# 64x64 products of a chunked delta rule on four quarters of the TensorE array, with half of the heads held on the other partitions

## The chip, the core and the metric

One core of a Trainium2 chip runs the whole program. Its engines work side by side and are told here by the names the profile uses: PE (TensorE matmuls; PEld are its weight loads), DVE (VectorE), ACT (ScalarE), POOL (GpSimd), and SP, which here only issues DMAs. The metric is the device time of one execution in microseconds, lower is better. The kernel before takes 1697.08 us, the median of three runs between 1696.71 and 1698.99.

## The reference

One layer of a decoder: 256 prompt tokens and 8 x 4 sample tokens (288 columns together) go through one wide projection, a gated convolution, a gated DeltaNet mixer with 8 heads of 128, merge gates, an output projection, and a feed-forward of width 8192, all in fp32. The part that the change touches is the chunked delta rule of the prompt, 4 chunks of 64 tokens for each head:

```python
M = jnp.where(strict, jnp.einsum('nbhid,nbhjd->nbhij', kb, kc) * decay, 0.0)
T = lax.linalg.triangular_solve(eye + M, jnp.broadcast_to(eye, M.shape),
                                left_side=True, lower=True, unit_diagonal=True)
u = T @ (vc * bc)
w = T @ (kb * jnp.exp(gcum)[..., None])
attn = jnp.einsum('nbhid,nbhjd->nbhij', qc, kc) * decay
...
def step(S, xs):
    qd, kd, u_c, w_c, a_c, gl = xs
    v_new = u_c - w_c @ S
    o = qd @ S + a_c @ v_new
    S = S * jnp.exp(gl)[..., None] + jnp.einsum('bhcd,bhce->bhde', kd, v_new)
    return S, o
```

M, T and attn are 64x64 for each chunk and head; S is 128x128 for each head.

## The kernel before

**The main stream.** Every large weight matrix is read in blocks of 512 KB. A block is split into a rounded part `hi` (ACT, line 179) and a remainder `lo` (DVE, line 186, recorded at line 140, the line of the helper `tt`), three blocks ahead of its use, and PE then issues 24 matmuls of 288 or 290 columns (lines 206 to 208), which the text calls big matmuls. All of this is in program order; there is no scheduler that moves work.

**The side work.** The gates, the delta rule `gdn(G)` for the heads 4G to 4G+3, and the decode step `sample()` are generators. Before each block's 24 big matmuls the main loop lets `side()` run to its next `yield`, and then, if there is one, the generator in `aux`. Whatever these issue to PE stands between two blocks of big matmuls, and PE takes it in that order. So every `yield` marks one block of distance.

**Tiles of the delta rule.** The four heads of a group are hh = 0 to 3, par = hh % 2 and p = hh // 2. `rows[par]` is partitions 0-63 or 64-127: a head with par = 0 keeps its 64 tokens on the lower half, one with par = 1 on the upper. `q` numbers chunk and p (q = 2c + p), 8 in all, so that a [128, 8, 64] tile holds the 64x64 matrices of 4 chunks and 4 heads.

**The steps that matter here**, for each of the two groups:

- Lines 1033 to 1040: the products K K^T and K Q^T into two banks, 32 matmuls.
- `pairs` (lines 1089 to 1093): 16 products of 64x64x64, the weights and moving data on the same half of the partitions that the result goes to. It is called six times in the inversion (lines 1114 to 1128): for s = 8, 16, 32 first `nM` with `Tm` into `px`, ACT copies that to `X`, and one block later `X` with `U` into `pq`, from which DVE updates `U`. Behind the second one at s = 8 and 16 PE also issues `states_of` (line 1081).
- Lines 1129 and 1130: `U` is spread into `U128`, and line 1049 does the same for `aT`: [128, 8, 128] tiles with the two heads' 64x64 matrices on the diagonal and zeros elsewhere, so that one 128x128 product serves two heads.
- The loop over the chunks c (lines 1235 to 1276): line 1240 (kq with S), line 1252 (`U128` with v, two 128x128x128 products, one bank `p2`), one or two blocks later line 1260 (`kdec` with v, the update of S, into two banks `p3`) and line 1263 (`aT` with v, the output, into a third bank `p4`). DVE or ACT empties each.
- `sample()` runs beside this loop for a while; its lines 1210 to 1214 do, for each head in a block of its own, two 512-column matmuls into fresh banks, each added into `S0` by DVE.

**PSUM.** `gtile()` hands out banks of [128, 512] from a pool of four. Each new tile waits until the tile that held its bank before has been read for the last time. Since PE works in order, a matmul that waits for a bank holds up everything behind it.

Of the kernel before, what the change touches and what calls it, by code (L numbers as in the profile page):

```python
# [103 lines left out]
def hybrid_kernel(ctx: ExitStack, tc: tile.TileContext, A):  # L104
# [34 lines left out]
    def tt(out, a, b, op):  # L139
        dve.tensor_tensor(out=out, in0=a, in1=b, op=op)  # L140
# [787 lines left out]
    def gdn(G):  # L928
# [31 lines left out]
        kst, qst = (kqs[:, u].rearrange("p h b t -> p (h b t)") for u in range(2))  # L960
        rows = (slice(0, 64), slice(64, 128))

        for c in range(4):
            kt = gtile()
            kv = kt.rearrange("p (h c) -> p h c", h=4)
            for hh in range(4):
                pe.transpose(kv[:, hh, :], kq[:, hh, c].rearrange("p s x -> p (s x)"), ident)  # L967
            s2 = sqr[:, 512 * (c % 2):512 * (c % 2) + 512].rearrange("p (h c) -> p h c", h=4)
            act.activation(s2, kv, AF.Square)
            for par in range(2):  # L970
                act.copy(kdec[rows[par], c], kv[rows[par], par::2, :])
# [6 lines left out]
        for par in range(2):  # L978
            act.copy(ssv[rows[par], 0], red[rows[par], :, par::2])
            act.copy(ssv[rows[par], 1], red[rows[par], :, 1 - par::2])  # L980
        sp2 = gtile()
# [29 lines left out]
        rk = rn[:, 0:8].rearrange("p (c r) -> p c r", c=4)  # L1011
        kdr = T([P, 4, 2], "kdr")
        brk = T([P, 4, 2], "brk")
        nbr = T([P, 4, 2], "nbr")
        tt(kdr, G_["kd"][:, :, pr], rk, MUL)
        tt(brk, G_["beta"][:, :, pr], rk, MUL)
        stt(nbr, brk, -1.0, rk, MUL, MUL)
        sc = T([P, 4], "sc")
# [11 lines left out]
        kdf = kdec.rearrange("p c r x -> p (c r) x")  # L1030
        tt(kdf, kdf, bc(qc(kdr), P), MUL)
        yield
        kkp, kqp = gtile(), gtile()
        for c in range(4):
            for hh in range(4):
                par = hh % 2
                q = (c * 2 + hh // 2) * 64
                ks_ = kq[:, hh, c, par, :]
                pe.matmul(kkp[rows[par], q:q + 64], ks_, ks_, start=True, stop=True)
                pe.matmul(kqp[rows[par], q:q + 64], ks_, kq[:, hh, c, 1 - par, :], start=True, stop=True)  # L1040
        nM = T([P, 8, 64], "gl")
# [46 lines left out]

        def pairs(out, a, b):
            for q in range(8):  # L1090
                for par in range(2):
                    r = rows[par]
                    pe.matmul(out[r, q * 64:q * 64 + 64], a[r, q, :], b[r, q, :], start=True, stop=True)  # L1093

# [11 lines left out]
        for j in range(1, 8):  # L1106
# [3 lines left out]
           cst("mask8").rearrange("p (b j) -> p b j", b=8).unsqueeze(1).to_broadcast([P, 8, 8, 8]), MUL)  # L1110
        dve.transpose(out=Tf, in_=Uf)
        for _ in range(3):
            yield
        for s in (8, 16, 32):
            px = gtile()
            pairs(px, nM, Tm)
            act.copy(X, px.rearrange("p (q c) -> p q c", c=64))
            yield
            pq = gtile()
            pairs(pq, X, U)  # L1120
            dve.copy_predicated(U, bmid(msk(s), 8), pq.rearrange("p (q c) -> p q c", c=64))
            if s < 32:
                dve.transpose(out=Tf, in_=Uf)
            if s < 32:
# [20 lines left out]
        def sample():  # L1145
# [41 lines left out]
            tt(vr, vtr.rearrange("p (h d) -> p h d", h=4), bc(rsc[:, 1], P), MUL)  # L1187
            v3 = pl.tile([P, 4, P], F32R, tag="U", name=nm("v3"))
            lows(v3, vr, 1)
# [45 lines left out]
        for c in range(4):  # L1235
            blk, half = c // 2, c % 2
            if c:
# [8 lines left out]
                for par in range(2):  # L1246
                    r = rows[1 - par]
                    tt(o[r, c], p1[r, par::2, :], bc(G_["egs"][r, c, pr], P), MUL)
                yield
            p2 = gtile()  # L1250
            for p in range(2):
                pe.matmul(p2[:, p * P:(p + 1) * P], U128[:, 2 * c + p, :], v[:, c, p, :], start=True, stop=True)  # L1252
            tt(v[:, c], p2[:, 0:256].rearrange("p (r x) -> p r x", r=2), bc(brk[:, c, :], P), MUL)
            yield
            if c == 0 or G == 0:
                yield
            p3, p4 = [gtile()[:, 0:256].rearrange("p (h c) -> p h c", h=2) for _ in range(2)], gtile()
            for hh in range(4):
                r = rows[hh % 2]
                pe.matmul(p3[hh % 2][:, hh // 2, :], kdec[r, c, hh // 2, :], v[r, c, hh // 2, :],  # L1260
                          start=True, stop=True)
            for p in range(2):
                pe.matmul(p4[:, p * P:(p + 1) * P], aT[:, 2 * c + p, :], v[:, c, p, :], start=True, stop=True)  # L1263
            p4v = p4[:, 0:256].rearrange("p (r x) -> p r x", r=2)
            if c == 0:
                for par in range(2):
                    act.copy(S[:, par::2, :], p3[par])
                act.copy(o[:, c], p4v)
            else:
                for hh in range(4):  # L1270
                    stt(S[:, hh, :], S[:, hh, :], G_["egl"][:, blk, 4 * G + hh, half:half + 1],
                        p3[hh % 2][:, hh // 2, :], MUL, ADD)
                tt(o[:, c], o[:, c], p4v, ADD)
            yield
# [22 lines left out]
        for u in range(2):  # L1297
            pt = gtile()
            for w in range(4):
                pe.transpose(pt[:, w * P:(w + 1) * P], of[:, 4 * u + w, :], ident)  # L1300
            pv = pt.rearrange("p (c r s x) -> p s c r x", c=2, r=2, s=2)
            for par in range(2):
                act.copy(gd["ao"][:, 1, 4 * G + par:4 * G + 4:2, P * u:P * u + P].rearrange("p r (c x) -> p c r x", c=2),
                         pv[:, 1 - par])
        yield
# [187 lines left out]
```

## Time and profile before

| | |
|---|---|
| median of three runs | 1697.08 us |
| the profiled execution's own time | 1699.71 us |
| its span, first to last instruction | 1697.9 us |
| mean granted TensorE clock over the span | 0.995 |
| DVE busy | 1011.1 us (60%) |
| ACT busy | 734.5 us (43%) |
| POOL busy | 130.6 us (8%) |

The page's first part gives the busy time of each engine, the second the same in 40 slices, the fourth the chain of work that ended last, and the fifth groups of equal instructions. Three more views are used below. The timeline lists instructions in order of start (start, duration, engine, line, operation, tile names, shapes, count), with the idle time of the engine before it and what ended it in brackets. The windows give the busy time, the granted clock and the DMA share of a stretch. The waits name who waited for whom. An fp32 matmul of the program shows as two records on PE in the trace, a weight load beside each; transposes and the big matmuls (fp32r) show as one.

### The profile page before, as it was taken

To read this page: it belongs to the slowest core of one execution; us is meant where nothing else is said; L and a number is where in the kernel's file an instruction comes from. 1 tells how busy PE (TensorE), PEld (TensorE's weight loads), DVE (VectorE), ACT (ScalarE), POOL (GpSimd) and SP (SyncE) were. 2 spreads that over 40 slices of the span, in tenths; PEclk is the share of its full clock that TensorE was granted. 3 is DMA by queue.
4 is the path that set the end of the run, shared out by engine and by line. 5 is a ranking of instruction groups with operands and counts; after the bars stand their busy time and mean duration, and the time that the engine had idled before them with its cause. 6 is when DMAs were issued, how large, how long until landed. Compare 5 with 4: busy or idle time off the path is not lost.

```text
span 1697.9 us, 31139 instructions
## 1 busy us (share of the span) xinstructions
PE 1685.4 (99%) x13073; PEld 1668.4 (98%) x13073; DVE 1011.1 (60%) x1304; ACT 734.5 (43%) x1068; POOL 130.6 (8%) x224
## 2 busy tenths in 40 slices
PE   9999999999999999999999999999999999999998
PEld 8999999999999999999999999999999999999997
DVE  6687966757544444556788744565445654466565
ACT  5785526334543333344445533344334433344342
POOL 2222421123300000000010000000000000000000
PEclk9999999999999999999999999999999999999998
DMA  9564366436555555555565555555555555555552
GB/s 256 155 194 137 113 185 204 140 112 180 171 165 170 162 165 168 164 162 162 169 185 171 167 169 167 162 164 169 165 163 161 170 166 164 168 166 162 164 161 81
DMA packets 275097, 279.18 MB, mean 164 GB/s; under 512 B 13131, under 2 KB 270092, under 8 KB 274952
## 3 DMA queue, kind: packets, MB, share of 16 engines
q1 hardware_dynamic: 270414, 265.95, 52.4%
q0 software_dynamic: 4256, 11.12, 2.4%
q8 instruction: 102, 1.67, 0.4%
q14 instruction: 37, 0.30, 0.0%
q10 hardware_dynamic: 288, 0.13, 0.0%
HBM read 269.68 MB, written 7.48 MB: 163 GB/s over the span
## 4 chain that ended last, share of the span: by engine, by line
PE 98%; DVE 1%; POOL 0%; issue 0%; ACT 0%; POOLq 0%; ACTq 0%
PE acc L206 31%; PE acc L208 31%; PE acc L207 31%; PE g L1093 1%; PE g L1081 0%; PE g L774 0%; PE g L1240 0%; PE g L1260 0%; PE g L840 0%; PE g L1212 0%; DVE w L143 0%; PE g L1263 0%; PE g L609 0%; PE g L1252 0%; PE g L807 0%; PE g L967 0%
## 5 line engine op out<-in xcount | busy, mean ns | idle before, releaser
L140 DVE TENSOR_TENSOR lo<-raw,hi 128x1024 fp32r<-128x1024 f32 (+2 forms) x502 | 614.3, 1226 | 551.7 <-ACT hi L179 549.3
L179 ACT CAST hi<-raw 128x1024 fp32r<-128x1024 f32 x492 | 514.1, 1046 | 761.4 <-PE acc L207 700.1
L206 PE MATMUL acc<-xh,hi 128*128 128x288 f32 x1408 | 422.2, 300 | 0.0
L208 PE MATMUL acc<-xh,lo 128*128 128x288 f32 x1408 | 416.8, 296 | 0.0
L207 PE MATMUL acc<-xl,hi 128*128 128x288 f32 x1408 | 416.3, 296 | 0.0
L206 PE MATMUL acc<-dh,hi 128*128 128x290 f32 x1024 | 303.9, 297 | 0.0
L207 PE MATMUL acc<-dl,hi 128*128 128x290 f32 x1024 | 303.2, 296 | 0.0
L208 PE MATMUL acc<-dh,lo 128*128 128x290 f32 x1024 | 302.7, 296 | 0.0
L206 PE MATMUL acc<-hh,hi 128*128 128x288 f32 x1024 | 302.3, 295 | 0.0
L208 PE MATMUL acc<-hh,lo 128*128 128x288 f32 x1024 | 302.3, 295 | 0.0
L207 PE MATMUL acc<-hl,hi 128*128 128x288 f32 x1024 | 302.3, 295 | 0.0
L206 PEld LDWEIGHTS acc<-xh,hi 128*128 128x128 f32 x1408 | 265.5, 189 | 2.1 <-issue 0.7
L207 PEld LDWEIGHTS acc<-xl,hi 128*128 128x128 f32 x1408 | 265.7, 189 | 0.6
L208 PEld LDWEIGHTS acc<-xh,lo 128*128 128x128 f32 x1408 | 265.4, 189 | 0.4 <-DVE lo L140 0.2
L206 PEld LDWEIGHTS acc<-dh,hi 128*128 128x128 f32 x1024 | 193.6, 189 | 0.1
L208 PEld LDWEIGHTS acc<-dh,lo 128*128 128x128 f32 x1024 | 193.3, 189 | 0.0
L207 PEld LDWEIGHTS acc<-dl,hi 128*128 128x128 f32 x1024 | 193.3, 189 | 0.1
L207 PEld LDWEIGHTS acc<-hl,hi 128*128 128x128 f32 x1024 | 192.5, 188 | 0.0
L208 PEld LDWEIGHTS acc<-hh,lo 128*128 128x128 f32 x1024 | 192.3, 188 | 0.0
L206 PEld LDWEIGHTS acc<-hh,hi 128*128 128x128 f32 x1024 | 192.1, 188 | 0.0
L207 PE MATMUL acc<-ml,hi 128*128 128x288 f32 x256 | 75.6, 295 | 0.0
L208 PE MATMUL acc<-mh,lo 128*128 128x288 f32 x256 | 75.6, 295 | 0.0
(407 smaller groups left out, 1627.5 us busy)
## 6 DMA issues: line engine op xcount, KB each, us to landing
raw<-in_w_in_dram SPq DMA_DIRECT2D x176, 512.0 KB, 3.7
raw<-in_w_up_dram SPq DMA_DIRECT2D x128, 512.0 KB, 3.8
raw<-in_w_down_dram SPq DMA_DIRECT2D x128, 512.0 KB, 3.6
raw<-in_w_o_dram SPq DMA_DIRECT2D x32, 512.0 KB, 3.7
raw<-in_w_a_out_dram SPq DMA_DIRECT2D x16, 512.0 KB, 3.7
raw<-in_w_b_out_dram SPq DMA_DIRECT2D x16, 512.0 KB, 3.6
S<-in_state_gdn_dram POOLq DMA_DIRECT2D x8, 512.0 KB, 8.6
out_dram<-S POOLq DMA_DIRECT2D x8, 512.0 KB, 4.9
```

Of the source, the lines that this page charges most:

```text
L140: dve.tensor_tensor(out=out, in0=a, in1=b, op=op)
L179: act.copy(his[i][:, k:k + step], raw[i][:, k:k + step])
L206: pe.matmul(o, wh, xh_, start=st, stop=False)
L207: pe.matmul(o, wh, xl_, start=False, stop=False)
L208: pe.matmul(o, wl, xh_, start=False, stop=en)
L1093: pe.matmul(out[r, q * 64:q * 64 + 64], a[r, q, :], b[r, q, :], start=True, stop=True)
```

## The change

- The matrices with p = 1 (odd q) are held on the other half of the partitions where that suits the array. `pairs` becomes `first` and `second`, which write the even q into one bank and the odd q into another. In `first` the products of odd q read one half of the partitions and write the other, so `X` has its odd q turned; `second` reads `X` there, together with `turn`, a copy of `U`'s odd q on the other half, and writes them back to their own.
- `other(out, src)` makes such a turned copy with two POOL instructions. It is called once for the decay matrix, three times for `U`, and once for small factors.
- `U128` is gone, and `aT` is [128, 8, 64]. The 128x128 products with two heads on the diagonal become four products of 64x64 with 128 columns (line 1276 and line 1290 of the new file); the ones of odd q cross to the other half. `v`, `o` and `kdec` hold p = 1 turned from there on, and turned back when heads are written to `ao`.
- `p4` is gone: the output products go into columns of the two banks `p3`. `p2` takes two banks in place of one.
- Several copies and multiplications that covered two heads at once are now two instructions, and the memsets of `U128` and `aT` go. `v3` gets a tag of its own.

```diff
-        U128 = T([P, 8, P], "U128")
-        aT = T([P, 8, P], "aT")
+        aT = T([P, 8, 64], "aT")
+        turn = T([P, 4, 64], "turn")
         gps.memset(kqm, 0.0)
-        for z in (U128, aT):
-            gps.memset(z, 0.0)
...
+        def other(out, src):
+            for par in range(2):
+                gps.tensor_copy(out[rows[1 - par]], src[rows[par]])
...
-        for par in range(2):
-            tt(aT[rows[par], :, 64 - 64 * par:128 - 64 * par],
-               kqp[rows[par]].rearrange("p (q c) -> p q c", c=64), Ef[rows[par]], MUL)
-        yield
+        other(turn, Ef[:, 1::2])
+        kq8 = kqp.rearrange("p (q c) -> p q c", c=64)
+        tt(aT[:, 0::2], kq8[:, 0::2], Ef[:, 0::2], MUL)
+        yield
+        tt(aT[:, 1::2], kq8[:, 1::2], turn, MUL)
         yield
...
-        def pairs(out, a, b):
+        def two():
+            return [gtile()[:, 0:256].rearrange("p (q c) -> p q c", c=64) for _ in range(2)]
+
+        def first(out, a, b):
             for q in range(8):
                 for par in range(2):
                     r = rows[par]
-                    pe.matmul(out[r, q * 64:q * 64 + 64], a[r, q, :], b[r, q, :], start=True, stop=True)
+                    pe.matmul(out[q % 2][rows[par ^ q % 2], q // 2, :], a[r, q, :], b[r, q, :], start=True, stop=True)
+
+        def second(out, a, b, bo):
+            for q in range(8):
+                for par in range(2):
+                    r = rows[par ^ q % 2]
+                    pe.matmul(out[q % 2][rows[par], q // 2, :], a[r, q, :], bo[r, q // 2, :] if q % 2 else b[r, q, :],
+                              start=True, stop=True)
...
         for s in (8, 16, 32):
-            px = gtile()
-            pairs(px, nM, Tm)
-            act.copy(X, px.rearrange("p (q c) -> p q c", c=64))
-            yield
-            pq = gtile()
-            pairs(pq, X, U)
-            dve.copy_predicated(U, bmid(msk(s), 8), pq.rearrange("p (q c) -> p q c", c=64))
+            px = two()
+            first(px, nM, Tm)
+            for u in range(2):
+                act.copy(X[:, u::2], px[u])
+            yield
+            pq = two()
+            second(pq, X, U, turn)
+            for u in range(2):
+                dve.copy_predicated(U[:, u::2], bmid(msk(s), 4), pq[u])
             if s < 32:
                 dve.transpose(out=Tf, in_=Uf)
+                other(turn, U[:, 1::2])
...
-        for par in range(2):
-            act.copy(U128[rows[par], :, 64 * par:64 * par + 64], U[rows[par]])
...
-            p2 = gtile()
+            p2 = [gtile()[:, 0:P] for _ in range(2)]
             for p in range(2):
-                pe.matmul(p2[:, p * P:(p + 1) * P], U128[:, 2 * c + p, :], v[:, c, p, :], start=True, stop=True)
-            tt(v[:, c], p2[:, 0:256].rearrange("p (r x) -> p r x", r=2), bc(brk[:, c, :], P), MUL)
+                for par in range(2):
+                    r = rows[par]
+                    pe.matmul(p2[p][rows[par ^ p]], U[r, 2 * c + p, :], v[r, c, p, :], start=True, stop=True)
+            for p in range(2):
+                tt(v[:, c, p], p2[p], kbt[:, 1, c, p:p + 1].to_broadcast([P, P]), MUL)
...
-            p3, p4 = [gtile()[:, 0:256].rearrange("p (h c) -> p h c", h=2) for _ in range(2)], gtile()
-            for hh in range(4):
-                r = rows[hh % 2]
-                pe.matmul(p3[hh % 2][:, hh // 2, :], kdec[r, c, hh // 2, :], v[r, c, hh // 2, :],
-                          start=True, stop=True)
+            p3 = [gtile().rearrange("p (h c) -> p h c", h=4) for _ in range(2)]
             for p in range(2):
-                pe.matmul(p4[:, p * P:(p + 1) * P], aT[:, 2 * c + p, :], v[:, c, p, :], start=True, stop=True)
-            p4v = p4[:, 0:256].rearrange("p (r x) -> p r x", r=2)
+                for b in range(2):
+                    r = rows[b]
+                    pe.matmul(p3[b][:, p, :], kdec[r, c, p, :], v[r, c, p, :], start=True, stop=True)
+            for p in range(2):
+                for b in range(2):
+                    r = rows[b]
+                    pe.matmul(p3[b][rows[1 - (b ^ p)], 2, :], aT[r, 2 * c + p, :], v[r, c, p, :],
+                              start=True, stop=True)
```

Three places show how the order of instructions changes. In the rows, a name's first number counts the tiles of that name in the program, and the brackets name the engines whose work the instruction waits for.

The first is PE at the first product of the inversion, group 0. Before (`g206` is `px`):

```order
L1093 MATMUL g206_1890<-xt170_1559,gl169_1558 64x64 [waits DVE_49]
L1093 MATMUL g206_1890<-xt170_1559,gl169_1558 64x64 x15
L1093 MATMUL g212_1949<-U171_1560,xt170_1559 64x64 [waits Activation_49]
L1093 MATMUL g212_1949<-U171_1560,xt170_1559 64x64 x15
```

The same place now (`g206` and `g207` are the two banks):

```order
L1104 MATMUL g206_1905<-xt170_1570,gl169_1569 64x64 [waits DVE_49]
L1104 MATMUL g206_1905<-xt170_1570,gl169_1569 64x64
L1104 MATMUL g207_1906<-xt170_1570,gl169_1569 64x64 [waits PE_49]
L1104 MATMUL g207_1906<-xt170_1570,gl169_1569 64x64
L1104 MATMUL g206_1905<-xt170_1570,gl169_1569 64x64 x2
L1104 MATMUL g207_1906<-xt170_1570,gl169_1569 64x64 x2
```

There are 16 products as before, two into one bank and two into the other in turn.

The second is PE at chunk 1 of group 0, where `sample()` issues its first two products (line 1212, now 1232) in the same gap between blocks. Before (`g290` and `g291` are `p3`, `g292` is `p4`):

```order
L1260 MATMUL g290_2661<-v238_2274,kdec119_1151 128x128 [waits DVE_49]
L1260 MATMUL g291_2662<-v238_2274,kdec119_1151 128x128 [waits PE_49]
L1260 MATMUL g290_2661<-v238_2274,kdec119_1151 128x128
L1260 MATMUL g291_2662<-v238_2274,kdec119_1151 128x128
L1263 MATMUL g292_2663<-v238_2274,aT115_1144 128x128 [waits PE_49]
L1263 MATMUL g292_2663<-v238_2274,aT115_1144 128x128
L1212 MATMUL g293_2675<-vm279_2575,kr3237_2273 128x512 [waits DVE_49,Pool_49]
L1212 MATMUL g294_2678<-vm279_2575,kr3237_2273 128x512 [waits DVE_49]
```

Now (`g297` and `g298` are the two banks `p3`; the last two rows stand one block later):

```order
L1286 MATMUL g298_2704<-v244_2303,kdec119_1149 128x128
L1290 MATMUL g297_2703<-v244_2303,aT114_1143 64x128
L1290 MATMUL g298_2704<-v244_2303,aT114_1143 64x128
L1290 MATMUL g297_2703<-v244_2303,aT114_1143 64x128
L1290 MATMUL g298_2704<-v244_2303,aT114_1143 64x128
L1232 MATMUL g299_2719<-vm286_2617,kr3243_2302 128x512 [waits PE_49,Pool_49]
L1232 MATMUL g300_2722<-vm286_2617,kr3243_2302 128x512 [waits DVE_49]
L1232 MATMUL g305_2762<-vm292_2660,kr3243_2302 128x512 [waits DVE_49,PE_49,Pool_49]
L1232 MATMUL g306_2765<-vm292_2660,kr3243_2302 128x512 [waits DVE_49,PE_49]
```

Before, this gap asked for five banks of a pool of four (290 to 294), so the last tile had to wait for the first of the same gap; now it asks for four (297, 298, 299, 300).

The third is POOL in the inversion of group 0, at s = 8 and the block behind it (`b` takes the spread keys for `states_of`, `stB` a convolution's history):

```order
L963 COPY turn115_1144<-U171_1571 64x256 [waits DVE_49,Pool_49]
L963 COPY turn115_1144<-U171_1571 64x256 [waits PE_49]
L1082 COPY b4112_1141<-kqs0_445 128x8x4 [waits PE_49,Pool_49]
L1082 COPY b4112_1141<-kqs0_445 128x8x4
L1082 COPY b4112_1141<-kqs0_445 128x8x4 [waits PE_49]
L1082 COPY b4112_1141<-kqs0_445 128x8x4
L266 MEMSET w1216_2015 128x3
```

Before, the four copies to `b` stood there without the two ahead of them.

More of the change, by code (lines that the diff above doesn't have):

```diff
@@ L970, in gdn @@
             for par in range(2):
-                act.copy(kdec[rows[par], c], kv[rows[par], par::2, :])
+                act.copy(kdec[rows[par], c, 0], kv[rows[par], par, :])
+                act.copy(kdec[rows[1 - par], c, 1], kv[rows[par], 2 + par, :])
             dve.tensor_reduce(out=red[:, c, :], in_=s2, axis=mybir.AxisListType.X, op=ADD)
@@ L979, in gdn @@
             act.copy(ssv[rows[par], 0], red[rows[par], :, par::2])
-            act.copy(ssv[rows[par], 1], red[rows[par], :, 1 - par::2])
+            for p in range(2):
+                act.copy(ssv[rows[par], 1, :, 1 - par ^ p], red[rows[par], :, 1 - par + 2 * p])
         sp2 = gtile()
@@ L1011, in gdn @@
         rk = rn[:, 0:8].rearrange("p (c r) -> p c r", c=4)
-        kdr = T([P, 4, 2], "kdr")
-        brk = T([P, 4, 2], "brk")
+        kdb = T([P, 2, 4, 2], "kdb")
+        kbt = T([P, 2, 4, 2], "kbt")
+        kdr, brk = kdb[:, 0], kdb[:, 1]
         nbr = T([P, 4, 2], "nbr")
@@ L1016, in gdn @@
         tt(brk, G_["beta"][:, :, pr], rk, MUL)
+        gps.tensor_copy(kbt[:, :, :, 0], kdb[:, :, :, 0])
+        other(kbt[:, :, :, 1], kdb[:, :, :, 1])
         stt(nbr, brk, -1.0, rk, MUL, MUL)
@@ L1039, in gdn @@
                 pe.matmul(kkp[rows[par], q:q + 64], ks_, ks_, start=True, stop=True)
-                pe.matmul(kqp[rows[par], q:q + 64], ks_, kq[:, hh, c, 1 - par, :], start=True, stop=True)
+                pe.matmul(kqp[rows[par ^ hh // 2], q:q + 64], ks_, kq[:, hh, c, 1 - par, :], start=True, stop=True)
         nM = T([P, 8, 64], "gl")
@@ L1114, in gdn @@
         for s in (8, 16, 32):
[L1115 to L1117 removed]
+            px = two()
+            first(px, nM, Tm)
+            for u in range(2):
+                act.copy(X[:, u::2], px[u])
             yield
[L1119 to L1121 removed]
+            pq = two()
+            second(pq, X, U, turn)
+            for u in range(2):
+                dve.copy_predicated(U[:, u::2], bmid(msk(s), 4), pq[u])
             if s < 32:
                 dve.transpose(out=Tf, in_=Uf)
+                other(turn, U[:, 1::2])
             if s < 32:
@@ L1187, in sample @@
             tt(vr, vtr.rearrange("p (h d) -> p h d", h=4), bc(rsc[:, 1], P), MUL)
-            v3 = pl.tile([P, 4, P], F32R, tag="U", name=nm("v3"))
+            v3 = pl.tile([P, 4, P], F32R, tag="v3", name=nm("v3"))
             lows(v3, vr, 1)
@@ L1271, in gdn @@
                     stt(S[:, hh, :], S[:, hh, :], G_["egl"][:, blk, 4 * G + hh, half:half + 1],
-                        p3[hh % 2][:, hh // 2, :], MUL, ADD)
-                tt(o[:, c], o[:, c], p4v, ADD)
+                        p3[hh % 2 ^ hh // 2][:, hh // 2, :], MUL, ADD)
+                for b in range(2):
+                    tt(o[:, c, b], o[:, c, b], p3[b][:, 2], ADD)
             yield
@@ L1302, in gdn @@
             for par in range(2):
-                act.copy(gd["ao"][:, 1, 4 * G + par:4 * G + 4:2, P * u:P * u + P].rearrange("p r (c x) -> p c r x", c=2),
-                         pv[:, 1 - par])
+                for p in range(2):
+                    act.copy(gd["ao"][:, 1, 4 * G + par + 2 * p, P * u:P * u + P].rearrange("p (c x) -> p c x", c=2),
+                             pv[:, 1 - par, :, par ^ p])
         yield
```

15 lines of the change are left out of this document (10 added, 5 removed).

## The prediction

> **What bounds the kernel now.** I read the page's busy times, then the chain that ended last, then who PE waited for.
>
> ```profile
> PE 1685.4 (99%) x13073; PEld 1668.4 (98%) x13073; DVE 1011.1 (60%) x1304; ACT 734.5 (43%) x1068; POOL 130.6 (8%) x224
> PE 98%; DVE 1%; POOL 0%; issue 0%; ACT 0%; POOLq 0%; ACTq 0%
> PE g L1212 <- DVE E L143: 3.0, 1, 3.0
> ```
>
> PE is busy for 99% of the span and is 98% of the chain, and its longest wait is one of 3.0 us. So the time is the sum of what PE issues, in its order. An instruction of DVE, ACT or POOL counts only where PE waits for it. I therefore price each piece of side work by what it pushes the big matmuls apart: from the start of the last big matmul before it to the start of the second one behind it, less two cadences. (The first one behind is already drawn out, the second is not.)
>
> The timeline of PE at the inversion of group 0:
>
> ```profile
> 141.14 0.29 PE L208 MATMUL acc<-xh,lo 128*128 128x288 f32 x1
> 141.36 1.15 PE L1093 MATMUL g<-xt,gl 64*64 64x64 f32 x32
> ...
> 142.68 0.29 PE L207 MATMUL acc<-xl,hi 128*128 128x288 f32 x1
> ...
> 145.59 0.29 PE L208 MATMUL acc<-xh,lo 128*128 128x288 f32 x1
> 145.81 1.15 PE L1093 MATMUL g<-U,xt 64*64 64x64 f32 x32
> 146.89 1.97 PE L1081 MATMUL g<-S,b 128*64 128x128 f32 x32
> ...
> 149.03 0.30 PE L207 MATMUL acc<-xl,hi 128*128 128x288 f32 x1
> ```
>
> The matmuls from 142.68 to 145.59 are the 2nd and the 24th of a block: 2.91 / 22 = 0.132 us each, a block 3.17, two cadences 0.265. The first `pairs` piece costs 142.68 - 141.14 - 0.265 = **1.28 us**. A record of it lasts 0.22 us (groups, below), so the 32 start within 1.15 - 0.22 = 0.93, one each 30 ns; 0.35 of the 1.28 is entering and leaving the small tile shape. The piece with `states_of` costs 149.03 - 145.59 - 0.265 = 3.18: 1.28, 32 records of 55 ns (1.97 - 0.27 = 1.70 for 31 steps, 1.76), and 0.14 for a third change of shape.
>
> The groups that give one record's own length, by form, the third the nearest to a 128x128 addition by DVE:
>
> ```profile
> L1093 PE MATMUL g<-xt,gl 64*64 64x64 f32 x192 | 6.9, 221 | 0.0
> L1252 PE MATMUL g<-v,U 128*128 128x128 f32 x32 | 4.9, 276 | 0.0
> L140 DVE TENSOR_TENSOR osm<-osm,g 128x128 f32<-128x128 f32 x2 | 0.6, 277 | 0.0
> L140 DVE TENSOR_TENSOR v<-g,brk 128x256 f32<-128x256 f32 x8 | 3.3, 414 | 0.0
> L140 DVE TENSOR_TENSOR xt<-g,gsw 64x256 f32<-64x256 f32 x12 | 5.0, 420 | 0.1
> ```
>
> And the timeline at the `U128` product of chunk 3 and at chunk 2's `kdec` and `aT` products:
>
> ```profile
> 241.93 0.29 PE L208 MATMUL acc<-xh,lo 128*128 128x288 f32 x1
> 242.06 0.61 PE L1252 MATMUL g<-v,U 128*128 128x128 f32 x4
> 242.64 0.29 PE L207 MATMUL acc<-xl,hi 128*128 128x288 f32 x1
> ...
> 230.20 0.29 PE L208 MATMUL acc<-xh,lo 128*128 128x288 f32 x1
> 230.42 0.72 PE L1260 MATMUL g<-v,kdec 64*128 64x128 f32 x8
> 231.07 0.71 PE L1263 MATMUL g<-v,aT 128*128 128x128 f32 x4
> 231.75 0.29 PE L207 MATMUL acc<-xl,hi 128*128 128x288 f32 x1
> ```
>
> The first costs 242.64 - 241.93 - 0.265 = 0.45: four records of 110 ns ((0.61 - 0.28) / 3) and no change of shape. The second costs 1.29. Half-height products (L1260) go at (0.72 - 0.27) / 7 = 64 ns a record and full ones at 110. So two halves of the array work at once wherever the trace has halves: the two column halves (L1081, 55 ns), the two row halves (L1260), and the two quarters on the diagonal (L1093: 30 ns against the 55 that half of 110 would be). Three or four quarters at once are nowhere in this trace.
>
> **The change, part by part.**
>
> *The inversion, 12 pieces.* The same 16 products now go round all four quarters. If each quarter works on its own, 32 records start in 0.47 in place of 0.93. Bounds: no gain (30 ns stays) and 0.93 / 2. I take the full half, because each pair of quarters that shares rows, shares columns, or shares neither is already seen to overlap in pairs. 12 x -0.465 = **-5.58 us**.
>
> *`U128`, 8 pieces.* Four records of 110 ns become eight of a quarter, and the piece now changes shape in and out: 0.35 + 8 x 0.0275 = 0.57 against 0.45, +0.12. If only two quarters overlap, 0.35 + 8 x 0.055 = 0.79, +0.34. 8 x 0.12 = **+0.96**.
>
> *`kdec` and `aT`, 8 pieces.* The 4 x 110 = 0.44 becomes 8 x 0.0275 = 0.22, and one more change of shape comes (0.14): -0.08, with two quarters only +0.14. 8 x -0.08 = **-0.64**.
>
> *K K^T and K Q^T* keep number, shape and banks; only the half of the columns is swapped for two heads: 0.
>
> *The wait for a bank.* Here lies the 3.0 us. PE's timeline, then DVE's at the same place, then the windows around it (span, PE, PEld, DVE, ACT, POOL, granted clock, DMA):
>
> ```profile
> 203.84 0.29 PE L208 MATMUL acc<-xh,lo 128*128 128x288 f32 x1
> 204.07 0.71 PE L1260 MATMUL g<-v,kdec 64*128 64x128 f32 x8
> 204.71 0.71 PE L1263 MATMUL g<-v,aT 128*128 128x128 f32 x4
> 205.18 0.47 PE L1212 MATMUL g<-vm,kr 128*128 128x512 f32 x1
> 208.63 0.80 PE L1212 MATMUL g<-vm,kr 128*128 128x512 f32 x1 [2.98 <-DVE E L143]
> 209.23 0.44 PE L206 MATMUL acc<-xh,hi 128*128 128x288 f32 x1
> ...
> 214.72 0.29 PE L208 MATMUL acc<-xh,lo 128*128 128x288 f32 x1
> 214.85 0.64 PE L1212 MATMUL g<-vm,kr 128*128 128x512 f32 x2
> 215.46 0.29 PE L207 MATMUL acc<-xl,hi 128*128 128x288 f32 x1
> ```
>
> ```profile
> 202.19 2.87 DVE L143 SCALAR_TENSOR_TENSOR w<-w,hw 128x312 f32<-128x312 f32 x3 [0.69 <-ACT w L271]
> 204.97 1.22 DVE L140 TENSOR_TENSOR lo<-raw,hi 128x1024 fp32r<-128x1024 f32 x1
> 206.11 1.70 DVE L143 SCALAR_TENSOR_TENSOR w<-w,hw 128x312 f32<-128x312 f32 x3
> 207.72 1.12 DVE L143 SCALAR_TENSOR_TENSOR E<-E,gexp,g 128x128 f32<-128x128 f32 x4
> ...
> 207.84:214.66 6.82, 6.03 (x24) 5.93 (x25) 4.71 (x8) 0.54 (x2) 2.77 (x2) 0.50 0.47 136
> ```
>
> The second L1212 takes the fifth bank of its gap and waits for the first to be emptied, by the updates of S, which DVE reaches at 207.72 behind a convolution. While PE stands still the granted clock falls to 0.50 for 6.82 us, and the 24 big matmuls behind it start (214.72 - 209.23) / 23 = 0.24 apart. The whole loss: from 203.84 to 214.72 pass 10.88; without the wait it would be 1.29, two L1212 (215.46 - 214.72 - 0.265 = 0.48) and a block of 3.17, so 4.94. **5.94 us are lost, twice the wait itself**; 5.94 - 2.98 = 2.96 of them go to the clock. In the new order this gap asks for four banks and both L1212 find one that was emptied a block earlier. What is late next: the L1212 pair one block on, at 205.18 + 0.48 + 3.17 = 208.8, whose banks are the two `p3`. DVE ends the four updates of S at 208.84 and then adds the two output halves, 0.28 each; and it comes up to 0.56 later than now, as since chunk 0 two evacuations (414 ns) are split into pairs of 277 and two of 420 into four. So PE waits from 0.3 (if DVE's idle 0.69 at 202 takes the splits up) to 2 us; I take 1.2, short of the idle time at which the clock fell. -5.94 + 1.2 = **-4.74** against the profiled execution.
>
> The clock may not have fallen in every execution: the profiled one lies 2.63 above the median of the runs, about the 2.96. The page can't settle that; I count half, 1.48, so against the median the term is **-3.26**, and with group 1 (below) the waits are -3.59. Both ends stay in the range.
>
> The Trainium skill, "TensorE: Matmul & The Clock Gate", "Part 1: The HAM clock gate", states that the clock is set by activity in a free-running window of about 3.4 us. The 6.82 us here agree with two such windows; by that rule it would hang on how the windows lie whether a wait of 2.98 us costs the 2.96 or not.
>
> In group 1 the same place is milder:
>
> ```profile
> 398.68 0.29 PE L208 MATMUL acc<-xh,lo 128*128 128x288 f32 x1
> 400.01 1.05 PE L1212 MATMUL g<-vm,kr 128*128 128x512 f32 x2
> 401.04 0.29 PE L207 MATMUL acc<-xl,hi 128*128 128x288 f32 x1
> ```
>
> 401.04 - 398.68 - 0.265 = 2.10 against 1.29 + 0.48: **-0.33** when that wait goes.
>
> *Off PE.* POOL gains some twenty copies and loses four memsets; `turn` is made at least one block (3.17) before DVE or PE reads it, ACT's two half copies of X also have a block, and `hi` and `lo` have three. I cost these at nothing; uncovered, a late `turn` would hold PE by about the length of its two copies, for which the nearest row is
>
> ```profile
> L985 POOL COPY vmh<-kqs 128x512 f32<-128x512 f32 x2 | 2.0, 1010 | 0.0
> ```
>
> 1 us, at six places at most.
>
> **Sum.** -5.58 + 0.96 - 0.64 - 4.74 - 0.33 = -10.33. The span of 1697.9 becomes 1687.6, and the profiled execution's 1699.71 becomes 1689.4. From the median, with half of the clock's share, -10.33 + 1.48 = -8.85 and 1697.08 - 8.85 = **1688.2 us**.
>
> **Rivals.**
>
> *Issue limits the quarters.* Records start no closer than the 30 ns seen, and the inversion gains nothing: -8.85 + 5.58 = -3.27, 1693.8. For it: no stretch of the trace is denser. Against: neighbouring records there start in couples that overlap, so 30 ns is a mean, not the least distance. The Trainium skill, "TensorE: Matmul & The Clock Gate", "Wait — 56ns, not 53.3ns?", gives a floor of about 25 ns from start to start: 32 x 25 = 0.80, an estimate of -1.6 us for the inversion.
>
> *Only two quarters at once.* Inversion 0, `U128` 8 x 0.34 = +2.7, `kdec` and `aT` 8 x 0.14 = +1.1, waits -3.59: +0.2, 1697.3. It would be so if products of different rows hinder each other in one bank, as the two quarters of each bank do in `first`. Against: L1093 already writes one bank from both row halves, at 30 ns. The Trainium skill, "TensorEngine Tiling (Array Packing)", "Gotcha 1: PSUM Pressure", says that different row tiles can't be in one bank at the same time; that row speaks against it, at least where the partitions differ.
>
> *Turning from one diagonal to the other drains the array (slower).* `first` and `second` do so 7 times a piece, `U128` and `aT` once. At the 0.14 of a change of shape, on top of two quarters at once: 12 x 0.98 + 8 x 0.48 + 8 x 0.28 - 3.59 = +14.3, 1711.3. It is slower than before by more than 0.2% from (3.4 - 0.2) / 100 = 32 ns a turn, there being 84 + 8 + 8 turns. Against: L1260 and L1081 change halves at every product and show no such gap.
>
> *The wait comes back one block on*, because DVE is 2.5 us behind there and PE arrives sooner: the waits stay as they were: -5.58 + 0.96 - 0.64 = -5.26, 1691.8.
>
> **How the numbers follow.** Forecast 0.62, issue limit 0.13, two quarters 0.09, drain 0.08, the wait comes back 0.08. 0.2% (3.4 us) is about what a measurement of this kernel can tell from no change. Faster: 0.62 + 0.08 and half of the issue limit, which lies on that edge, 0.765, say 0.77; same the other half and two quarters, 0.15; slower 0.08. The forecast's own ends are 1684.6 (the whole clock's share, none of the 1.2 left, the `U128` pieces at their old price) and 1690.5 (none of the clock's share, a wait of 2 us left); with the issue limit and the returning wait the range is 1684.0 to 1694.5, which leaves out two quarters and the drain, 0.17.
>
> **What would show it.** The two forms of 64x64 products with 64 columns at about 15 ns a record, pieces of 0.81 in place of 1.28; L1276 pieces near 0.57; L1212's successor without a bracket of 3 us and the granted clock at 1.00 from 200 to 225 us. Wrong would be 30 ns a record, gaps at every second product, or a new bracket on PE that names POOL `turn` or DVE.

## The result, and the profile after

The changed kernel takes **1690.09 us**, the median of five runs (1689.49 to 1690.27), against 1698.99 of five runs of the kernel before, three of them those that the prediction started from (1696.71 to 1700.1): a ratio of **0.9949** (95% interval 0.9935 to 0.9964). The forecast was 1688.2. The profiled execution went from 1699.71 to 1689.69, by 10.02; the sum of the prediction said 10.33.

The head of the page of the changed kernel, and the longest wait of its PE:

```profile
span 1687.9 us, 31377 instructions
PE 1676.5 (99%) x13137; PEld 1656.3 (98%) x13137; DVE 1011.4 (60%) x1336; ACT 735.8 (44%) x1102; POOL 138.5 (8%) x242
```

```profile
PE g L1232 <- DVE xt L140: 1.3, 1, 1.3
```

PE is still the whole chain. Its busy time fell by 8.9, and the wait of 3.0 us is gone; a new one of 1.3 stands in the same function (L1232 is the old L1212). DVE, ACT and POOL do slightly more work; the other waits in PE's list are those of before.

The timeline of its PE, at the first inversion product, at chunk 2's products of `kdec` and `aT`, and at chunk 3's product of `U`:

```profile
140.73 0.29 PE L208 MATMUL acc<-xh,lo 128*128 128x288 f32 x1
140.96 0.69 PE L1104 MATMUL g<-xt,gl 64*64 64x64 f32 x32
...
141.82 0.29 PE L207 MATMUL acc<-xl,hi 128*128 128x288 f32 x1
...
222.90 0.29 PE L208 MATMUL acc<-xh,lo 128*128 128x288 f32 x1
223.12 0.72 PE L1286 MATMUL g<-v,kdec 64*128 64x128 f32 x8
223.77 0.45 PE L1290 MATMUL g<-v,aT 64*64 64x128 f32 x8
...
224.38 0.30 PE L207 MATMUL acc<-xl,hi 128*128 128x288 f32 x1
...
234.56 0.29 PE L208 MATMUL acc<-xh,lo 128*128 128x288 f32 x1
234.79 0.45 PE L1276 MATMUL g<-v,U 64*64 64x128 f32 x8
...
235.41 0.29 PE L207 MATMUL acc<-xl,hi 128*128 128x288 f32 x1
```

With the prediction's measure (the two big matmuls around a piece, less 0.265), the inversion piece costs 141.82 - 140.73 - 0.265 = 0.82, the second 1.22, the third 0.58. The 32 records of the inversion start within 0.69 - 0.22 = 0.47, one each 15 ns, half of before.

The same view around chunk 1, where the wait was:

```profile
200.80 0.29 PE L208 MATMUL acc<-xh,lo 128*128 128x288 f32 x1
201.02 0.72 PE L1286 MATMUL g<-v,kdec 64*128 64x128 f32 x8
201.67 0.45 PE L1290 MATMUL g<-v,aT 64*64 64x128 f32 x8
202.05 0.74 PE L1232 MATMUL g<-vm,kr 128*128 128x512 f32 x2
...
202.75 0.29 PE L207 MATMUL acc<-xl,hi 128*128 128x288 f32 x1
...
205.67 0.29 PE L208 MATMUL acc<-xh,lo 128*128 128x288 f32 x1
207.28 0.70 PE L1232 MATMUL g<-vm,kr 128*128 128x512 f32 x2 [1.31 <-DVE xt L140]
...
207.95 0.29 PE L207 MATMUL acc<-xl,hi 128*128 128x288 f32 x1
```

Both L1232 of the first gap find their banks. One block on the next two wait 1.31 us for the banks of the updates: 207.95 - 205.67 - 0.265 = 2.02 where an undisturbed pair costs 0.48, so 1.54 us are lost. DVE at that place:

```profile
202.69 3.21 DVE L143 SCALAR_TENSOR_TENSOR w<-w,hw 128x312 f32<-128x312 f32 x3
205.82 1.11 DVE L143 SCALAR_TENSOR_TENSOR E<-E,gexp,g 128x128 f32<-128x128 f32 x4
206.85 0.48 DVE L140 TENSOR_TENSOR xt<-xt,g 128x128 f32<-128x128 f32 x2
```

The four updates of S, and behind them the two additions of the output halves (recorded as `xt`), end at 207.33. PE goes on at 207.28, when the first addition is done.

Why DVE is late here shows beside POOL's rows. The three convolution instructions ahead of the updates (`w`) took 1.70 us in the kernel before and take 3.21 here. The middle one alone takes 2.06 us, where the same one took 0.54 before. Meanwhile POOL runs the multiplication that spreads a coming head's `vm`:

```profile
203.26 2.06 DVE L143 SCALAR_TENSOR_TENSOR w<-w,hw 128x312 f32<-128x312 f32 x1
202.94 2.05 POOL L1221 TENSOR_TENSOR vm<-v,cf 128x1024 fp32r<-128x1024 f32 x1 [2.25 <-PE g L1232]
```

The same multiplication in the kernel before:

```profile
209.58 1.90 POOL L1201 TENSOR_TENSOR vm<-v,cf 128x1024 fp32r<-128x1024 f32 x1 [5.48 <-PE g L1212]
```

The multiplication waits until PE has read the old `vm`. Before, PE's own wait held it back until the updates were done (208.84). Now it starts at 202.94 and meets the convolution. In the twelve traces a convolution instruction of this form takes 0.53 to 0.78 us with no POOL multiplication beside it, and 1.2 to 2.2 us wherever one runs beside it for 1.2 us or more. Without the 1.52 us that were added here, DVE would end its additions at 205.81, and PE arrives at 205.97 (207.28 - 1.31): by this estimate no wait would be left. No run moves the multiplication away, so this cause is read from the rows and not tested by itself.

### The profile page after: what moved, and what is told of

Same layout as the page of the kernel before. It is cut to its first block, busy times and chain, and to the rows that moved or that the text cites. A ratio compares the mean times of both kernels' runs of the same rounds, so it can differ in the third digit from the quotient of the medians.

```text
span 1687.9 us, 31377 instructions
## 1 busy us (share of the span) xinstructions
PE 1676.5 (99%) x13137; PEld 1656.3 (98%) x13137; DVE 1011.4 (60%) x1336; ACT 735.8 (44%) x1102; POOL 138.5 (8%) x242
## 4 chain that ended last, share of the span: by engine, by line
PE 98%; DVE 1%; POOL 0%; issue 0%; ACT 0%; POOLq 0%; ACTq 0%
PE acc L206 31%; PE acc L208 31%; PE acc L207 31%; PE g L1089 0%; PE g L774 0%; PE g L1260 0%; DVE w L143 0%; PE g L1286 0%; PE g L1232 0%; PE g L840 0%; PE g L1110 0%; PE g L1104 0%; PE g L609 0%; PE g L807 0%; PE g L969 0%
```

## The experiments

Differences of 1 to 3 us in 1700 are at issue, so the medians of several runs stand beside the profile of one execution. The kernel before, run 21 times beside the first four kernels, has a median of 1698.73.

**The inversion alone.** The kernel before, with only the inversion on four quarters:

```diff
...
-            px = gtile()
-            pairs(px, nM, Tm)
-            act.copy(X, px.rearrange("p (q c) -> p q c", c=64))
+            px = two()
+            first(px, nM, Tm)
+            for u in range(2):
+                act.copy(X[:, u::2], px[u])
             yield
-            pq = gtile()
-            pairs(pq, X, U)
-            dve.copy_predicated(U, bmid(msk(s), 8), pq.rearrange("p (q c) -> p q c", c=64))
+            pq = two()
+            second(pq, X, U, turn)
+            for u in range(2):
+                dve.copy_predicated(U[:, u::2], bmid(msk(s), 4), pq[u])
```

> The kernel before with only the inversion on four quarters (two banks, turn in an idle part of rep4); U128, aT, p2, p3 and p4 as before. Theory (the gain is 12 inversion pieces at half of their records' time, and, apart from that, a bank that was short): pieces of 0.82 us in place of 1.28, 5.5 us less in all; the wait of some 3 us at line 1212's successor in group 0 stays, and with it the fall of the granted clock to 0.50. Profiled time about 1699.7 - 5.5 = 1694.2. Rival (the wait went because PE comes earlier or the other engines have less to do, not because of the banks): the wait is gone here too, about 1690.

Measured: 1692.51 (five runs, 1690.94 to 1694.33), ratio 0.9962 (0.9949 to 0.9976). The pieces are those of the changed kernel, 0.82 in place of 1.27 at all twelve places, which is 12 x 0.45 = 5.4 of the 6.2 us. The wait remains, as its longest wait shows:

```profile
PE g L1231 <- DVE E L143: 2.5, 1, 2.5
```

It is 0.4 shorter than before (2.55 for 2.98), and in this profile the clock fell for 3.41 us only (the last section). That is about the size of the rest, though the clock's share differs from run to run. So the inversion's term stands by itself.

**The outputs alone.** The kernel before, with only the two output products moved into the free half of the first of the updates' banks:

```diff
-            p3, p4 = [gtile()[:, 0:256].rearrange("p (h c) -> p h c", h=2) for _ in range(2)], gtile()
+            p3 = [gtile().rearrange("p (h c) -> p h c", h=4) for _ in range(2)]
...
-                pe.matmul(p4[:, p * P:(p + 1) * P], aT[:, 2 * c + p, :], v[:, c, p, :], start=True, stop=True)
+                pe.matmul(p3[0][:, 2 + p, :], aT[:, 2 * c + p, :], v[:, c, p, :], start=True, stop=True)
...
```

> The kernel before with only the output products (p4) moved into free columns of the first update bank; everything on two quarters and with U128 as before. Theory: the gap asks for four banks, the wait of 2.98 us goes, one of about 1 us comes a block later, the granted clock stays at 1.00: 4.5 to 5 us less than a run before that loses the clock, profiled time about 1695; pieces of the inversion stay at 1.28. Rival (DVE is late in any case, so the wait only moves by one block, with the clock): within 1 us of before, 1699.

Measured: 1695.56 (eleven runs, 1694.8 to 1696.22), ratio 0.998 (0.9971 to 0.9989). No product became cheaper here; what is gained is the wait alone. Its PE's timeline one block behind the place of the old wait:

```profile
208.23 0.29 PE L208 MATMUL acc<-xh,lo 128*128 128x288 f32 x1
210.10 0.80 PE L1212 MATMUL g<-vm,kr 128*128 128x512 f32 x2 [1.58 <-DVE E L143]
...
210.88 0.29 PE L207 MATMUL acc<-xl,hi 128*128 128x288 f32 x1
```

The wait of 2.98 became one of 1.58, a block later, and the granted clock stayed at 1.00. The piece costs 210.88 - 208.23 - 0.265 = 2.39, 1.91 over an undisturbed one, in place of 5.94. Here, too, a convolution instruction ahead of the updates is drawn out, to 2.18 us in place of 0.54, beside POOL's multiplication at 205.50.

**The outputs in banks of their own.** The changed kernel, with the output products taken out of the updates' banks again:

```diff
             p3 = [gtile().rearrange("p (h c) -> p h c", h=4) for _ in range(2)]
+            p4 = [gtile()[:, 0:P] for _ in range(2)]
...
-                    pe.matmul(p3[b][rows[1 - (b ^ p)], 2, :], aT[r, 2 * c + p, :], v[r, c, p, :],
+                    pe.matmul(p4[b][rows[1 - (b ^ p)]], aT[r, 2 * c + p, :], v[r, c, p, :],
...
```

> The changed kernel with the output products in two banks of their own again (six banks asked for in the gap at chunk 1). Theory: both line-1232 products of that gap wait for update banks that DVE empties 2.5 us late: a wait of 3 us or more, the granted clock falls to 0.50 behind it, 4 to 6 us more than the changed kernel, about 1694 to 1696; inversion pieces stay at 0.82. Rival (the wait had gone for another reason): 1690, as the changed kernel.

Measured: 1698.0 (eleven runs, 1695.29 to 1699.56), ratio 0.9992 (0.9983 to 1.0001), so the gain of the whole change is gone, more of it than was expected. Its waits:

```profile
PE g L1232 <- DVE E L143: 3.9, 2, 3.2
PE g L1212 <- DVE E L143: 1.8, 1, 1.8
...
PE g L1194 <- ACT E L1294: 0.8, 2, 0.6
```

The wait at chunk 1 is back at 3.2 us, and a second one of 1.8 arose in group 1; the two outputs take two banks here, where the kernel before had one. Behind the first the clock fell for 6.82 us, behind the second for 3.41. So the products on four quarters with two banks of their own for the outputs are worth almost nothing here: what the array saves, PE gives back in waiting for banks.

**The order of the products.** The changed kernel, with all even q ahead of all odd q in `first` and `second`, and then in turns of two:

```diff
-            for q in range(8):
+            for q in (0, 2, 4, 6, 1, 3, 5, 7):
```

> The changed kernel with the products of the inversion issued all even q first, then all odd q: the same 16 products, but one diagonal of the array for the first half of the list and the other for the second. If each quarter draws from a queue that holds the whole piece, pieces stay near 0.82 us. If PE looks ahead only a few instructions, the diagonals run one after the other and a piece costs up to 1.28 us, 5.5 us more in all, about 1695.

```diff
-            for q in range(8):
+            for q in (0, 2, 1, 3, 4, 6, 5, 7):
```

> The changed kernel with its 16 products in the order of q 0, 2, 1, 3, 4, 6, 5, 7: two even ones, then two odd ones. The kernel that issued all even ones first took 0.76 us from its first record to its last (1.11 a piece), the changed kernel 0.48 (0.82). Theory: PE issues in order, but a few records ahead of the quarter that is busy; if some four records wait in all, twos take 0.54 (0.89 a piece, +0.8 us in all); if each quarter has a queue of two of its own, 0.50 (0.84, +0.2 us). Rival: what costs is each turn from one diagonal to the other; then the three turns here cost more than the single one of all even ones first, and a piece is over 1.11.

Measured, one run each: 1694.03 and 1690.49. The pieces cost 1.11 at all twelve places (0.29 more, 3.5 us in all) and 0.87. The start of such a piece in PE's timeline, even then odd:

```profile
145.97 0.51 PE L1110 MATMUL g<-U,xt 64*64 64x64 f32 x10
146.26 0.27 PE L1110 MATMUL g<-turn,xt 64*64 64x64 f32 x2
```

and in the changed kernel:

```profile
144.96 0.27 PE L1110 MATMUL g<-U,xt 64*64 64x64 f32 x2
145.01 0.27 PE L1110 MATMUL g<-turn,xt 64*64 64x64 f32 x2
```

The first record of an odd product (those with `turn`) starts 0.05 us behind the first even one in the changed kernel, and 0.29 behind it where the even ones go first, when 10 of their 16 have started. So PE issues in order and some records ahead of a busy quarter, and two quarters stand idle until the order reaches their products. No cost of a turn from one diagonal to the other shows: the order with most turns is the fastest. With four records waiting in all, turns of two were to take 0.89, with two for each quarter 0.84; 0.87 lies between and doesn't settle how the waiting is organised.

**The two terms that were costs.** The changed kernel with the block matrices `U128` kept for the product with `v`; with the second head of `sample()` one block later in group 0; with both; and as it is, beside them:

```diff
...
-            for p in range(2):
-                for par in range(2):
-                    r = rows[par]
-                    pe.matmul(p2[p][rows[par ^ p]], U[r, 2 * c + p, :], v[r, c, p, :], start=True, stop=True)
+            for p in range(2):
+                pe.matmul(p2[:, p * P:(p + 1) * P], U128[:, 2 * c + p, :], v[:, c, p, :], start=True, stop=True)
...
```

> The changed kernel, but the product of U with v goes by the block matrices U128 again (two 128x128 products in one bank, one DVE multiplication). Theory: those pieces cost what their records and their changes of shape cost, so each of the 8 falls from 0.58 back to 0.45 (the first of each group from 0.58 to about 0.61 or less), about -1.0 us in all: 1689.1 against the changed kernel's 1690.09. The wait one block on stays, as its banks are still those of the updates; it is 0.1 shorter, since DVE has one multiplication of 420 ns there in place of two of 277. Rival: what counts is the number of banks and not the records, so that p2's second bank matters; then the wait moves to another L1232 by over 0.5 us and the time is 1690 or more.

```diff
                 yield
+                if G == 0 and hh == 1:
+                    yield
                 for j in range(2):
```

> The changed kernel with one more yield ahead of the second head of sample() in group 0, so that its matmuls reach the two banks one block (3.2 us) later. Theory: the 1.54 us that the piece at 207.28 loses (2.02 in place of 0.48) is only PE arriving before DVE has emptied the updates' banks, and a block is longer than that; it goes, nothing else moves by 0.2 us, 1688.5. Rival: the wait moves on with the banks, to the next two L1232 behind L1260 or behind L1276, and the time stays at 1690.

> Both of these edits in one kernel: the block matrices U128 for the product of U with v, and the second head of sample() one block later. Theory: they act at different places of PE and add up, -1.0 and -1.5: 1687.5, below both kernels. Rival: with one bank less asked for by p2 the order of the four banks shifts, a wait of 0.5 to 1.5 us appears at another place, 1688.5 to 1689.

> The changed kernel as it is, beside the others on the same chip, as the measure for differences of 1 us. Theory: no wait of PE in it is long enough to cost the clock, so its runs lie within 0.8 us of each other, 1689.5 to 1690.3, all at a clock of 0.998 or 0.997, while those of the kernel before spread over 3 us with the clock. Rival: the spread of the kernel before has nothing to do with its 3 us wait; then these runs spread over 2 us or more as well, given as many.

The kernel before, nine runs beside these, has a median of 1698.62.

| | median of five runs | range | ratio to before (95%) |
|---|---|---|---|
| changed kernel again | 1690.32 us | 1689.95 to 1690.36 | 0.995 (0.9937 to 0.9964) |
| `U128` kept | 1689.25 us | 1689.02 to 1689.54 | 0.9945 (0.9932 to 0.9957) |
| second head later | 1688.56 us | 1688.51 to 1689.47 | 0.9942 (0.993 to 0.9955) |
| both | **1687.52 us** | 1687.12 to 1688.45 | 0.9935 (0.9923 to 0.9948) |

With `U128` kept, its PE at chunk 3 (235.62 - 234.91 - 0.265 = 0.45, as before the change), and the wait one block behind chunk 1:

```profile
234.91 0.29 PE L208 MATMUL acc<-xh,lo 128*128 128x288 f32 x1
235.04 0.60 PE L1279 MATMUL g<-v,U 128*128 128x128 f32 x4
...
235.62 0.29 PE L207 MATMUL acc<-xl,hi 128*128 128x288 f32 x1
```

```profile
PE g L1237 <- DVE xt L140: 1.4, 1, 1.4
```

The product term is right. The wait was to be 0.1 shorter and is 0.1 longer; the cheaper piece ahead of it (0.67 in place of 0.80) lets PE arrive 0.1 earlier, which was not thought of. In the kernel with the later head there is no such wait, although the convolution instruction takes 2.06 us there too: PE comes a block later. Where the two matmuls now stand, behind L1262, they find their banks:

```profile
209.17 0.29 PE L208 MATMUL acc<-xh,lo 128*128 128x288 f32 x1
209.30 1.05 PE L1262 MATMUL g<-E,kq 128*128 128x128 f32 x8
210.11 0.71 PE L1234 MATMUL g<-vm,kr 128*128 128x512 f32 x2
...
210.79 0.29 PE L207 MATMUL acc<-xl,hi 128*128 128x288 f32 x1
```

210.79 - 209.17 - 0.265 = 1.36, as in the changed kernel (1.37). Against the changed kernel beside them, the two gains are 1.1 and 1.8 us, and together 2.8: they add up, and the kernel with both is the fastest of all.

**The kernel before once more**, for a second profile of it.

> The kernel before as it is, for a second profile of it. Theory: the wait of the fifth bank is 2.9 to 3.0 us again, but the clock stays at 0.50 for 0, 3.4 or 6.8 us, and the time follows it: about 1696.8, 1698.5 or 1699.7. Rival: the clock is at 0.50 for 6.8 us in every execution, and the spread of the times comes from somewhere else.

Measured: 1698.93. Its PE at the wait:

```profile
203.49 0.29 PE L208 MATMUL acc<-xh,lo 128*128 128x288 f32 x1
...
208.30 0.50 PE L1212 MATMUL g<-vm,kr 128*128 128x512 f32 x1 [3.00 <-DVE E L143]
...
213.22 0.29 PE L208 MATMUL acc<-xh,lo 128*128 128x288 f32 x1
```

From big matmul to big matmul pass 9.73, against 10.88 in the first profile and 4.94 without a wait. The wait is the same, 3.00 and 2.98, but 1.79 and not 2.96 went to the clock, which stayed at 0.50 for 3.41 us and not for 6.82.

## Why the prediction was right, by its own steps

| term | forecast | profile |
|---|---|---|
| inversion, 12 pieces | -5.58 | -5.41 |
| `U128`, 8 pieces | +0.96 | +0.93 |
| `kdec` and `aT`, 8 pieces | -0.64 | -0.52 |
| wait at chunk 1, group 0 | -4.74 | -4.40 |
| the same place, group 1 | -0.33 | -0.35 |
| sum | -10.33 | -9.75 |

The right column is each piece's price after less its price before, all by the same measure. The span itself fell by 10.0, so some 0.25 us lie outside these pieces.

- **Each quarter works on its own**: right, and shown alone by the first experiment. The records start 15 ns apart where 14.7 were assumed.
- **The change of shape** (0.14, and 0.35 to go in and out), read from one piece of before, carried over to new ones: 0.58 for `U`, where 0.57 was forecast, and 1.22 for `kdec` with `aT`, where 1.205 was. Keeping `U128` takes the one back, as it should.
- **The wait goes because this gap asks for four banks**: right, and shown from both sides, by the outputs alone moved in and by the outputs moved out again.
- **What is late next**: the right place and the right banks, but for another reason, and mis-sized by 0.34: 1.54 lost where 1.2 was taken out of 0.3 to 2. The prediction made DVE late by its split evacuations; by that reckoning its additions end at most 5.9 us behind the start of the `kdec` products (208.84, two halves of 0.28 and up to 0.56 of splits, from 204.07). They end 6.3 behind it (207.33 - 201.02), and 1.52 of that are the convolution instruction beside POOL's multiplication. Without these it would be 4.8, less than the 5.1 of the kernel before (208.75 + 0.41 - 204.07), so the splits show nothing. That 1.2 came near 1.54 is luck. One block's distance takes the wait away, as the later head shows.
- **Work off PE at nothing**: right for the new work; no wait of PE in the changed kernel's list names POOL or `turn`. It overlooked old work that moves: with PE's wait gone, POOL's `vm` multiplication runs earlier, and by the rows it is what makes DVE late. The prediction's list of signs would call a new wait of PE that names DVE wrong; there is one, at the place where its own sum had 1.2.
- **From the profiled execution to the median**: here lie the 1.9 us between 1688.2 and 1690.09. The prediction took the median of three runs, 1697.08, as its base and counted half of the clock's share back. Two of the three were low, and the kernel before lies at 1698.73 in 21 runs, which is 1.65 of the 1.9. The change in the median, 1698.99 to 1690.09, is -8.90 against -8.85 forecast; from 1698.73 it would be -8.64, so that the two agree to 0.05 is partly luck. 1690.09 still lies within the forecast's own ends, 1684.6 to 1690.5, near the upper one.

The Trainium skill's floor of about 25 ns from start to start ("TensorE: Matmul & The Clock Gate", "Wait — 56ns, not 53.3ns?") would have made the inversion pieces 0.35 + 0.80 = 1.15, an estimate. The pieces cost 0.82, so between different quarters it doesn't hold; the measurement decides. Nor does "TensorEngine Tiling (Array Packing)", "Gotcha 1: PSUM Pressure", in the form that different row tiles can't be in one bank at once: in `first` and `second` both row halves write each bank, which takes a record each 30 ns, while those of one quarter start 58 ns apart.

Of the rivals, two quarters only, the issue limit and a drain at each turn fall with the 0.82 and with the order of the products. The wait that comes back one block on did come, but with 1.54 of the 5.94 us that it had cost, and by way of POOL.

## What to carry to other kernels

Put small products so that neighbours in program order go to different quarters of the array (a piece took 0.82 us so, and 1.11 with one diagonal ahead of the other); price a piece as its records plus its changes of tile shape, which is why four 128x128 records beat eight quarter records for `U`. Where PE is the bound, look for the gap that asks for one bank more than the pool has: here it was worth 4.4 us in the profile beside 5.4 of the faster inversion, and alone, by the medians, 3.2 beside 6.2. Then ask what the removed wait sets free: here a POOL multiplication came earlier, DVE became late beside it, and a `yield` in the right place was worth 1.8 us more. And before a forecast counts from a median of three, look at how far the runs spread and why.

## What was not expected of the hardware

The clock's share is a draw. Of the 30 runs of the kernel before in the two rounds of timing, by their mean granted clock over the span:

| clock | runs | time |
|---|---|---|
| 0.998 | 3 | 1696.79 to 1697.20 us |
| 0.997 | 8 | 1697.61 to 1698.97 us |
| 0.996 | 10 | 1698.28 to 1698.73 us |
| 0.995 | 9 | 1699.27 to 1699.90 us |

The first row fits the profiled execution's 1699.71 less the 2.96 that its clock cost, 1696.75. The ten runs of the changed kernel, 0.997 or 0.998 all of them, spread over 0.87 us.

In the traces the clock changes in steps of 3.41 us. Windows cut at these steps (length, then busy time of PE, PEld, DVE, ACT, POOL, then the granted clock), of the first profile of the kernel before:

```profile
204.43:207.84 3.41, 1.22 (x13) 0.79 (x9) 3.30 (x7) 1.50 (x5) 0.00 (x0) 1.00 0.17 40
207.84:211.25 3.41, 2.62 (x10) 2.52 (x11) 3.41 (x8) 0.54 (x2) 1.67 (x1) 0.50 0.40 134
211.25:214.66 3.41, 3.41 (x16) 3.41 (x15) 1.30 (x1) 0.00 (x0) 1.10 (x2) 0.50 0.53 138
```

of the second profile of it:

```profile
205.45:208.86 3.41, 0.56 (x3) 0.52 (x4) 3.34 (x10) 0.68 (x4) 0.00 (x0) 1.00 0.51 145
208.86:212.27 3.41, 3.41 (x16) 3.41 (x15) 3.07 (x3) 0.00 (x0) 2.77 (x2) 0.50 0.03 8
```

of the kernel with outputs in their own banks, at its wait of 3.2 and, in the last two rows, at the one of 1.8:

```profile
201.20:204.61 3.41, 1.70 (x22) 1.17 (x20) 3.29 (x6) 1.93 (x4) 0.27 (x2) 1.00 0.24 83
...
382.10:385.51 3.41, 1.61 (x21) 1.25 (x20) 3.41 (x10) 0.69 (x1) 2.73 (x2) 1.00 0.15 25
385.51:388.92 3.41, 3.41 (x16) 3.41 (x15) 1.09 (x1) 0.00 (x0) 2.85 (x2) 0.50 0.69 200
```

and of the kernel with `U128` kept, at its wait of 1.4 (cut by the same step, counted from the first change of the clock in its trace):

```profile
204.67:208.08 3.41, 2.00 (x15) 1.78 (x14) 3.37 (x9) 1.47 (x3) 0.84 (x1) 1.00 0.46 148
208.09:211.50 3.41, 3.41 (x26) 3.37 (x26) 3.41 (x6) 0.00 (x0) 2.12 (x2) 1.00 0.19 55
```

A window at the full clock in which PE was busy for up to 1.70 of its 3.41 us was followed by one at 0.50, one with 2.00 was not. So a wait of 1.8 us can cost the clock when it falls into one window, and one of 3 us costs one window or two, by where it is cut: in the first profile the last 0.79 of it reached into the next window, and the clock stayed low for another. Cut in the middle, it would leave (6.82 - 3.0) / 2 = 1.9 us busy in each of two windows, an estimate, which lies between 1.70 and 2.00. The three runs at 0.998 would fit with its costing nothing then, but no trace shows such a run. The Trainium skill, "TensorE: Matmul & The Clock Gate", "Part 1: The HAM clock gate", has the free-running window of about 3.4 us, and the traces agree (3.41); it has the clock fall after a window that is idle, and here windows half busy were enough. Where between 1.70 and 2.00 the edge lies, and whether it is a count of busy time at all, these few windows don't settle.
